# One block of attention, RWKV and feed-forward on one core: ascending queries, a fused output projection, weight sums made once

## The chip, the core and the metric

The kernel is one program on one core of a Trainium2 chip. The metric is the device time of one execution in microseconds (us); the change is timed against the kernel before on the same chip. The core's engines are PE (TensorE, matrix multiply), DVE (VectorE), ACT (ScalarE), POOL (GpSimd) and SP (SyncE, which only issues transfers here). Each takes its instructions in the order in which they stand in its queue; between engines there are semaphores. TensorE runs at one of two clocks, 2.4 or 1.2 GHz; the profile gives the granted clock of a stretch as a share of the full one.

## What is computed

2048 tokens of width 1024 pass through one block, all in float32:

```
u   = rmsnorm(x, attn_norm_pre)
p   = u @ w_in                            # queries, keys, values, gates; RWKV columns
o   = concat(forgetting_attention(p_fox), # 8 heads of 64, causal, log-gate bias
             rwkv7_time_mix(p_rwkv))      # 8 heads of 64, delta-rule state scan
h   = x + rmsnorm(o @ w_out, attn_norm_post)
z   = rmsnorm(h, ffn_norm_pre)
f   = (silu(z @ ffn_w_gate) * (z @ ffn_w_up)) @ ffn_w_down      # inner width 2816
out = h + rmsnorm(f, ffn_norm_post)
```

## The kernel before

Every float32 product is made of three matrix multiplications in a reduced format: an operand x is split into a high part (an ACT cast) and a low part (a DVE or POOL subtraction), and `mm3` adds high·high, high·low and low·high in PSUM (L78, L79 and L80). The big matrices are multiplied in blocks of two by two with seven products instead of eight, so that sums and differences of blocks have to be formed by DVE and POOL and split too. The Python code is written as generators that are woven together; a scheduler then orders the instructions of every engine, so that the order in an engine's queue is not that of the code.

The program runs in stages, told by the line of their TensorE work:

- Until about 805 us: input projection, its norms, and the operands of the RWKV scan.
- 805 to 1604 us (`phase_b`): the RWKV recurrence, woven with `attention`. Attention works head by head in units of 256 queries, J from 7 down to 0; unit J needs keys 0 to 256·(J+1). Keys (Ks), values (Vs) and gate sums (ng) come in four segments of 512 keys a head, the last segment first (L864 to L872). The heads' results go to a DRAM tensor, scr_mixT (L977 for attention, L780 for RWKV).
- 1604 to 1849 us (`Mix`): the output projection `passes` in four passes: columns 0 to 511 of the first 1024 tokens, columns 512 to 1023 of the same, then these two for the other tokens. Only one half of w_out is on chip, so that it is loaded and split three times (L1035 to L1046), and every tile of scr_mixT is loaded and split twice (`load`, L1049). A tile's result goes from PSUM through ACT (L1081) to a DRAM tensor, scr_mix. `norm` (L1087) reads a tile of 128 tokens back, makes both norms with an inverse square root by Newton steps on DVE (L61 to L63), adds x on POOL (L1111), writes h, and transposes z on TensorE (npt, L1121) into DRAM (scr_z). The first eight tiles are normed beside the projection, the last eight as side work of gate and up.
- 1849 to 2749 us (`Ffn.quad`): 44 quads of gate or up, each of 7 products of 12 multiplications (gp), 22 for each half of the tokens. `wprep` loads and splits the weights of the next quad (fraw, wh, wl); `zprep` builds the operands za, zb, zc of a half from scr_z, for the first half in `start` and `open`. The products of the quad go through four PSUM banks. The inner activations are written to a DRAM tensor, scr_hid (L1381).
- 2749 to 3299 us (`down`): for each half of the tokens, five chunks of two row pairs, and in a chunk 7 products × 4 tiles (dps) that are added up on DVE (L1574; those of the first chunk are copied by ACT, L1571), then a last pair (L1600) and the final norm. `down_prep` makes a chunk's operands: four loads of 1 MB each (L1436; two of scr_hid, two of w_down), sums s1 to s4 of the activations and t1 to t4 of the weights on DVE (L1482), then high parts (ACT, L1474) and low parts (POOL or DVE, L1476).

The sums t1 to t4 depend on the weights alone, and are formed for each half again:

```
            add(t1, b12, b11, ALU.subtract)     # L1498 and on: 2 adds a call
            ops(s1, t1)
            add(t3, b22, b12, ALU.subtract)
            ops(s3, t3)
```

Of the kernel before, what the change touches and what calls it, by code (L numbers as in the profile page):

```python
# [10 lines left out]
F32 = mybir.dt.float32  # L11
# [820 lines left out]
def attention(k, tc, ctx, scr):  # L832


# [23 lines left out]
    def load_head(h):  # L858
# [5 lines left out]
        def loads():  # L864
            for sgm in range(NS - 1, -1, -1):
# [144 lines left out]
class Mix:  # L1010


    def __init__(m, k, tc, ctx, ins, scr):
        m.k, m.nc, m.ins, m.scr = k, tc.nc, ins, scr
        m.pw = ctx.enter_context(tc.tile_pool(name="e_w", bufs=1, side="right"))
        m.pr = ctx.enter_context(tc.tile_pool(name="e_r", bufs=1, side="right"))
        m.w = [None] * NJ
        m.d = 0
        m.low = itertools.cycle([m.nc.gpsimd])
        m.rot = [(m.pr, f"r{i}") for i in range(3)]  # L1020

    def open(m, tc, ctx):

        m.pm = ctx.enter_context(tc.tile_pool(name="e_m", bufs=2, side="right"))
        m.pn = ctx.enter_context(tc.tile_pool(name="e_n", bufs=1, side="right"))
        m.low = itertools.cycle([m.nc.vector, m.nc.gpsimd])
        m.rot += [(m.pm, f"r{i}") for i in range(3, 8)]
# [6 lines left out]

    def weights(m):  # L1035

        nc = m.nc
        c = slice(m.d * 512, (m.d + 1) * 512)
        for j in range(NJ):
            h = m.pw.tile([128, 512], F32R, tag=f"wh{j}", name="ewh")  # L1040
            l = m.pw.tile([128, 512], F32R, tag=f"wl{j}", name="ewl")
            t = m.r([128, 512])
            nc.sync.dma_start(out=t, in_=m.ins["w_out"][0][j * 128:(j + 1) * 128, c])
            nc.scalar.copy(h, t)
            next(m.low).tensor_tensor(l, t, h, op=ALU.subtract)
            m.w[j] = h, l  # L1046
            yield

    def load(m, tt):  # L1049
        nc = m.nc  # L1050
        t = slice(tt * 128, (tt + 1) * 128)
        mh = m.pm.tile([128, NJ, 128], F32R, tag="mh", name="emh")
        ml = m.pm.tile([128, NJ, 128], F32R, tag="ml", name="eml")
        for i in range(2):
            c = slice(i * 4, (i + 1) * 4)
            r = m.r([128, 4, 128])
            nc.sync.dma_start(out=r, in_=m.scr["mixT"][i * 512:(i + 1) * 512, t].rearrange("(j p) t -> p j t", p=128))
            nc.scalar.copy(mh[:, c], r)
            next(m.low).tensor_tensor(ml[:, c], r, mh[:, c], op=ALU.subtract)
        return mh, ml  # L1060

    def passes(m, psum, done):

        nc = m.nc
        n = m.k.T // 256
        for i, half in enumerate((0, 0, 1, 1)):
            if i % 2 == 1:
                m.d = 1 - m.d
                for _ in m.weights():
                    pass  # L1070
            c = slice(m.d * 512, (m.d + 1) * 512)
            nxt = m.load(half * n)
            for tt in range(half * n, (half + 1) * n):
                mh, ml = nxt
                if tt + 1 < (half + 1) * n:
                    nxt = m.load(tt + 1)
                ps = psum.tile([128, 512], F32, tag="e", name="eps")
                for j, (wh, wl) in enumerate(m.w):
                    mm3(nc, ps, mh[:, j, :], ml[:, j, :], wh, wl, j == 0, j == NJ - 1)
                o = m.r([128, 512])  # L1080
                nc.scalar.copy(o, ps)  # L1081
                nc.scalar.dma_start(out=m.scr["mix"][tt * 128:(tt + 1) * 128, c], in_=o)
                if i % 2 == 1:
                    done[0] = tt + 1
                yield

    def norm(m, tt, pool, psum, bufs=1):  # L1087
# [3 lines left out]
        a = pool.tile([128, D], F32, tag="na", name="na", bufs=bufs)  # L1091
        nc.sync.dma_start(out=a, in_=scr["mix"][t, :])
        ss = pool.tile([128, 1], F32, tag="nss", name="nss", bufs=bufs)
        rs = pool.tile([128, 1], F32, tag="nrs", name="nrs", bufs=bufs)

        def factor():
            junk = pool.tile([128, D], BF16, tag="nr", name="njunk", bufs=2 * bufs)
            nc.scalar.activation(junk, a, AF.Square, accum_out=ss)
            nc.vector.tensor_scalar(ss, ss, 1.0 / D, NORM_EPS, op0=ALU.mult, op1=ALU.add)
            rsqrt(nc, pool, rs, ss, "nq")  # L1100

        factor()
        yield
        for d in range(2):
            c = slice(d * 512, (d + 1) * 512)
            g = pool.tile([128, 512], F32, tag="nr", name="ng", bufs=2 * bufs)
            nc.sync.dma_start(out=g, in_=m.ins["attn_norm_post"][0][c].partition_broadcast(128))
            nc.vector.scalar_tensor_tensor(a[:, c], a[:, c], rs, g, op0=ALU.mult, op1=ALU.mult)
            x = pool.tile([128, 512], F32, tag="nr", name="nx", bufs=2 * bufs)
            nc.sync.dma_start(out=x, in_=m.ins["x"][0, t, c])  # L1110
            nc.gpsimd.tensor_tensor(a[:, c], a[:, c], x, op=ALU.add)  # L1111
            yield
        nc.gpsimd.dma_start(out=scr["h"][t, :], in_=a)
        factor()
# [556 lines left out]
```

## Time and profile before

| | us |
|---|---|
| median of 3 runs | 3307.99 (3302.31 to 3308.15) |
| the profiled execution | 3300.75 |
| its span, first to last instruction | 3299.0 |
| TensorE busy in the span | 3032.2 (92%) |
| VectorE busy | 2434.5 (74%) |
| ScalarE busy | 1584.9 (48%) |
| GpSimd busy | 1383.9 (42%) |

The mean granted clock of TensorE was 0.961. An engine's busy share is an average over stages with different limits. A view that cuts the span into windows shows for each stage how long each engine worked in it; where TensorE stands below its window, the rows of its timeline tell in brackets how long it had been idle before an instruction, and which engine or transfer ended that. A row of the windows holds start and end, length, busy time (and number of instructions) of PE, PEld (TensorE's weight loads), DVE, ACT and POOL, then the granted clock, the busy share of the sixteen transfer engines and the GB/s that they moved. A group of instructions gives its count, its busy time with the mean of one in ns, and the idle time before its instructions with what ended it.

### The profile page before, as it was taken

How to read it: one execution, taken by the hardware profiler on the slowest of the kernel's cores; microseconds unless marked ns; L12 is line 12 of the kernel's file. 1: busy time of each engine (PE TensorE's matmuls, PEld its weight loads, DVE VectorE, ACT ScalarE, POOL GpSimd, SP SyncE). 2: the span in 40 equal slices, each digit the busy share in tenths (PEclk: the TensorE clock that was granted, in tenths of full speed). 3: DMA queues.
4: the chain of work that ended last, by engine and by line, in shares of the span. 5: the costliest groups of instructions: out<-in, count | busy, mean ns of one | idle time of the engine just before them, and what ended most of it. 6: DMA issues, size and time to landing. Idle time of an engine off the chain costs nothing. (4 is left out here: it accounts for less than half of the span.)

```text
span 3299.0 us, 48970 instructions
## 1 busy us (share of the span) xinstructions
PE 3032.2 (92%) x16913; PEld 2511.0 (76%) x16913; DVE 2434.5 (74%) x5129; ACT 1584.9 (48%) x3256; POOL 1383.9 (42%) x1031
## 2 busy tenths in 40 slices
PE   7999999998999999999797699999899999996895
PEld 5777777777888889988676578888788887774674
DVE  6876777675677777777545867877865657999898
ACT  5444534433677777777444434333333335333432
POOL 3444444443111111111334434444533336887786
PEclk9999999999999999999898899999999999998998
DMA  4766656668433333332377634442322224231321
GB/s 131 193 148 183 178 159 167 154 174 229 119 110 120 105 113 108 107 106 62 97 224 241 218 106 138 139 136 89 128 77 83 84 90 160 102 128 48 131 103 77
DMA packets 463629, 434.09 MB, mean 132 GB/s; under 512 B 138148, under 2 KB 379862, under 8 KB 461334
## 3 DMA queue, kind: packets, MB, share of 16 engines
q1 hardware_dynamic: 432262, 390.52, 39.0%
q10 hardware_dynamic: 24208, 20.52, 2.1%
q0 software_dynamic: 6912, 19.93, 2.0%
q8 instruction: 134, 2.20, 0.3%
q14 instruction: 113, 0.93, 0.1%
HBM read 304.11 MB, written 126.75 MB: 131 GB/s over the span
## 5 line engine op out<-in xcount | busy, mean ns | idle before, releaser
L255 POOL TENSOR_TENSOR wl<-wraw,wh 128x1024 fp32r<-128x1024 f32 (+1 forms) x108 | 263.4, 2443 | 286.9 <-ACT wh L254 283.7
L1231 POOL TENSOR_TENSOR wl<-fraw,wh 128x512 fp32r<-128x512 f32 x132 | 184.9, 1402 | 462.1 <-ACT wh L1227 447.5
L1476 POOL TENSOR_TENSOR dop<-draw,dop 128x512 fp32r<-128x512 f32 x210 | 331.5, 1610 | 101.2 <-ACT dop L1474 57.3
L1227 ACT CAST wh<-fraw 128x512 fp32r<-128x512 f32 x308 | 187.2, 618 | 387.7 <-PE gp L79 206.0
L78 PE MATMUL mm<-uh,wh 128*128 128x512 f32 (+1 forms) x864 | 347.2, 403 | 0.0
L80 PE MATMUL mm<-uh,wl 128*128 128x512 f32 (+1 forms) x864 | 344.4, 399 | 0.0
L79 PE MATMUL mm<-ul,wh 128*128 128x512 f32 (+1 forms) x864 | 343.4, 397 | 0.0
L78 PE MATMUL dps<-dop 128*128 128x512 f32 x624 | 251.2, 410 | 62.9 <-ACT acc L1571 26.2
L1474 ACT CAST dop<-draw 128x512 fp32r<-128x512 f32 x280 | 155.5, 620 | 231.8 <-DVE draw L1482 160.2
L79 PE MATMUL dps<-dop 128*128 128x512 f32 x624 | 248.9, 400 | 1.4 <-POOL dop L1476 1.4
L80 PE MATMUL dps<-dop 128*128 128x512 f32 x624 | 246.0, 398 | 0.1
L78 PE MATMUL gp<-za,wh 128*128 128x512 f32 x528 | 210.4, 398 | 21.4 <-ACT za L1227 15.5
L976 POOL TENSOR_TENSOR ot<-ot,rb 64x256 f32<-64x256 f32 x64 | 46.4, 726 | 428.2 <-ACT rb L975 428.2
L1231 DVE TENSOR_TENSOR wl<-fraw,wh 128x512 fp32r<-128x512 f32 x176 | 153.7, 873 | 86.6 <-ACT wh L1227 73.7
L955 DVE TENSOR_TENSOR tl<-pt,th 128x512 fp32r<-128x512 f32 (+1 forms) x280 | 163.2, 591 | 73.2 <-ACT th L953 69.6
L79 PE MATMUL gp<-za,wh 128*128 128x512 f32 x528 | 208.4, 395 | 1.2 <-DVE za L1231 1.2
L80 PE MATMUL gp<-za,wl 128*128 128x512 f32 x528 | 208.6, 395 | 0.0
L78 PEld LDWEIGHTS dps<-dop 128*128 128x128 f32 x624 | 121.0, 194 | 107.8 <-DVE acc L1574 35.0
L1482 DVE TENSOR_TENSOR draw<-draw 128x512 f32<-128x512 f32 x160 | 198.0, 1254 | 6.5 <-POOL dop L1476 6.0
L909 DVE CUSTOM_DVE_ANT_0 P<-S,ng 128x512 f32<-128x512 f32 (+2 forms) x320 | 183.6, 605 | 24.8 <-PE pt L947 13.9
L78 PEld LDWEIGHTS mm<-uh,wh 128*128 128x128 f32 (+1 forms) x864 | 164.6, 191 | 41.3 <-issue 3.5
L920 ACT ACTIVATE P<-P,nmx 128x896 f32<-128x896 f32 (+7 forms) x248 | 187.5, 761 | 14.4 <-DVE nmx L914 14.1
(376 smaller groups left out, 8554.1 us busy)
## 6 DMA issues: line engine op xcount, KB each, us to landing
wraw<-in_w_in SPq DMA_DIRECT2D x104, 512.0 KB
fraw<-in_ffn_w_gate SPq DMA_DIRECT2D x22, 1024.0 KB
fraw<-in_ffn_w_up SPq DMA_DIRECT2D x22, 1024.0 KB
scr_hid<-s SPq DMA_DIRECT2D x22, 1024.0 KB
draw<-scr_hid SPq DMA_DIRECT2D x22, 1024.0 KB
draw<-in_ffn_w_down SPq DMA_DIRECT2D x22, 1024.0 KB
scr_a<-A SPq DMA_DIRECT2D x16, 1280.0 KB
A<-scr_a SPq DMA_DIRECT2D x64, 320.0 KB
```

Of the source, the lines that this page charges most:

```text
L78: nc.tensor.matmul(out, lhsT=wh, rhs=xh, start=first, stop=False)
L79: nc.tensor.matmul(out, lhsT=wh, rhs=xl, start=False, stop=False)
L80: nc.tensor.matmul(out, lhsT=wl, rhs=xh, start=False, stop=last)
L255: nc.gpsimd.tensor_tensor(wl[:, :, 0:m], raw[:, :, 0:m], wh[:, :, 0:m], op=ALU.subtract)
L909: nc.vector.tensor_tensor_reduce(out=P[:, c0:c0 + n], in0=S[:, 0:n], in1=ng[c0 // 512][:, 0:n], op0=ALU.add, op1=ALU.max, scale=1.0, scala ...
L920: nc.scalar.activation(P[:, x0:x1], P[:, x0:x1], AF.Exp, bias=nmx, accum_out=ls[:, qi, i:i + 1])
L955: nc.vector.tensor_tensor(tl[:, w[0], w[1]], pt[:, w[0], w[1]], th[:, w[0], w[1]], op=ALU.subtract)
L1227: f.nc.scalar.copy(h, x)
L1231: e.tensor_tensor(l[:, c], x[:, c], h[:, c], op=ALU.subtract)
L1474: f.nc.scalar.copy(r[0][p][i], x)
L1476: e.tensor_tensor(r[1][p][i], x, r[0][p][i], op=ALU.subtract)
L1482: V.tensor_tensor(o[p], x[p], y[p], op=op)
```

## The change

Four parts are changed; the counts are of instructions in the built programs.

1. `attention`: units go from J = 0 to 7, segments are loaded from the first on; of the first head two segments are requested ahead, the others at J = 2 and 3, those of the next head at J = 4 and 6.
2. `Mix`: both halves of w_out are held on chip, split once (`others` brings the second half in during the first tiles). `project` takes two tiles of tokens at a time through both halves; each tile of scr_mixT is loaded and split once. The result stays in SBUF (na); squares are summed by ACT from PSUM; scr_mix is gone. The inverse root is ACT's square root with one Newton step (`rsqrt2`). All 16 tiles are normed beside the projection. The projection has PSUM banks of its own, three for eps and one for npt.
3. `Ffn`: gate, up and down use eight PSUM banks in turn (`bank`). The weights of the first quad are prepared in `open`. A new generator, `column_sums`, forms t1 to t4 for the five chunks of w_down once, as side work of gate and up: 20 units, each of two loads of 256 KB, four POOL sums of 128x256 elements and one store of 512 KB, the transfers too issued by POOL.
4. `down_prep`: the DVE sums t1 to t4 are gone, 80 of 160 (L1482). `column_loads` reads the seven weight operands of a chunk, 512 KB each, from w_down or from the stored sums (scr_wt), up to six ahead.

```diff
-            for J in range(NJU - 1, -1, -1):
+            for J in range(NJU):
...
-        for _ in units[0].hd.loads:
-            pass
+        next(units[0].hd.loads)
+        next(units[0].hd.loads)
...
-            if u is not None and u.J * QB % 512 == 0 and i + NJU < len(units):
+            if u is not None and u.J in (2, 3):
+                next(u.hd.loads)
+            elif u is not None and u.J in (4, 6) and i + NJU < len(units):
                 next(units[i + NJU].hd.loads)
...
+    def project(m, ready):
+        n = m.k.T // 128
+        ops = {tt: m.load(tt) for tt in range(2)}
+        others = m.others()
+        for p in range(0, n, 2):
...
+            for d in range(2):
+                for tt in (p, p + 1):
...
+                    ps = m.ps.tile([128, 512], F32, tag="e", name="eps")
...
+                    for j, (wh, wl) in enumerate(m.w[d]):
+                        mm3(nc, ps, mh[:, j, :], ml[:, j, :], wh, wl, j == 0, j == NJ - 1)
...
+                    nc.scalar.activation(junk, ps, AF.Square, accum_out=a[tt][1][:, d:d + 1])
+                    nc.scalar.copy(a[tt][0][:, c], ps)
+                    if d == 1:
+                        ready.append((tt, *a[tt]))
...
+    def norm(m, tt, a, s2):
...
+            nc.vector.scalar_tensor_tensor(a[:, c], a[:, c], rs, m.g[:, c], op0=ALU.mult, op1=ALU.mult)
+            nc.gpsimd.tensor_tensor(x[:, c], a[:, c], x[:, c], op=ALU.add)
+            nc.scalar.activation(junk, x[:, c], AF.Square, accum_out=s2[:, d:d + 1])
...
+    def bank(f, new=True):
+        f.nps += 1
+        return f.ps[f.nps % 2 if new else 0].tile([128, 512], F32, tag="g", name="gp")
...
+    def column_sums(f):
+        for fp in range(f.NP - 1):
+            for q in range(2):
+                x = f.pc.tile([128, 2, 2, 256], F32, tag="cs", name="csum")
+                for j in range(2):
+                    nc.gpsimd.dma_start(out=x[:, j], in_=w[fp, :, j]...)
+                yield
+                G.tensor_tensor(b11, b12, b11, op=ALU.subtract)
+                G.tensor_tensor(b12, b22, b12, op=ALU.subtract)
+                G.tensor_tensor(b22, b22, b11, op=ALU.subtract)
+                G.tensor_tensor(b21, b21, b22, op=ALU.subtract)
+                nc.gpsimd.dma_start(out=f.scr["wt"][fp, :, :, q * 256:(q + 1) * 256], ...)
+                yield
...
+            if q > 0:
+                side.append(itertools.islice(sums, 1 + (q % 2)))
...
+    def column_loads(f, seq):
+            for b in ("b11", "b21", 0, 1, 3, "b22", 2):
...
+                f.nc.sync.dma_start(out=x, in_=src.rearrange("f p c -> p f c"))
...
-            add(t1, b12, b11, ALU.subtract)
-            ops(s1, t1)
+            ops(s1)
...
-                pool, tag = ((f.psd, "d"), (f.ps, "g"))[nps[0] % 2]
+                ps = f.bank()
```

Where attention ends and the output projection begins, TensorE's queue held this before (O is attention's result, gp here the RWKV output gate, eps the projection, emh the split tile of scr_mixT):

```order
L78 MATMUL gp<-xl_16171,g1h 128x512
L79 MATMUL gp<-xl_16173,g1h 128x512
L80 MATMUL gp<-xl_16171,g1l 128x512
L778 MATMUL gp<-xl_16175,g2s 128x512
L965 MATMUL O<-th,Vs 128x256
L965 MATMUL O<-th,Vs 128x128
L969 MATMUL O<-ident,rl 64x128 x2
L78 MATMUL eps<-ewh,emh 128x512
L79 MATMUL eps<-ewl,emh 128x512
```

Now it holds this there (yT is the transpose that ends the recurrence):

```order
L964 MATMUL O<-th,Vs 128x128
L964 MATMUL O<-tl,Vs 128x128
L968 MATMUL O<-ident,rl 64x128 x2
L769 MATMUL yT<-ident,yg 128x128 x8
L78 MATMUL eps<-ewh,emh 128x512
L79 MATMUL eps<-ewl,emh 128x512
L80 MATMUL eps<-ewh,eml 128x512
```

The projection's first rows now stand ahead of the gate's, which come among them; before, the gate's last rows stood ahead of attention's last result.

VectorE's queue in a middle chunk of the down product held this before (draw is the result of a sum, dop a low part, acc the adding up):

```order
L1574 TENSOR_TENSOR acc<-dps,acc 128x512 x4
L1476 TENSOR_TENSOR dop<-draw,dop 128x512
L1482 TENSOR_TENSOR draw<-draw 128x512 x2
L1574 TENSOR_TENSOR acc<-dps,acc 128x512 x2
L1482 TENSOR_TENSOR draw<-draw 128x512
L1574 TENSOR_TENSOR acc<-dps,acc 128x512 x2
L1476 TENSOR_TENSOR dop<-draw,dop 128x512
L1482 TENSOR_TENSOR draw<-draw 128x512 x3
L1574 TENSOR_TENSOR acc<-dps,acc 128x512 x5
L1476 TENSOR_TENSOR dop<-draw,dop 128x512
L1574 TENSOR_TENSOR acc<-dps,acc 128x512 x2
L1482 TENSOR_TENSOR draw<-draw 128x512
```

Now it holds this in such a chunk:

```order
L1570 TENSOR_TENSOR draw<-draw 128x512
L1652 TENSOR_TENSOR acc<-gp,acc 128x512
L1570 TENSOR_TENSOR draw<-draw 128x512
L1652 TENSOR_TENSOR acc<-gp,acc 128x512 x2
L1564 TENSOR_TENSOR dop<-draw,dop 128x512
L1652 TENSOR_TENSOR acc<-gp,acc 128x512
L1570 TENSOR_TENSOR draw<-draw 128x512
L1652 TENSOR_TENSOR acc<-gp,acc 128x512
L1570 TENSOR_TENSOR draw<-draw 128x512
L1652 TENSOR_TENSOR acc<-gp,acc 128x512 x2
L1564 TENSOR_TENSOR dop<-draw,dop 128x512
L1652 TENSOR_TENSOR acc<-gp,acc 128x512 x4
```

The sums between the additions to acc came in groups of one to three, and come singly now.

SP's queue at the start of the down product held this before (scr_hid<-s is the store of the last activations):

```order
L1381 DMA scr_hid<-s 128x2x1024
L1436 DMA draw<-in_ffn_w_down 128x2x1024
L1436 DMA draw<-scr_hid 128x2x1024
L1436 DMA draw<-in_ffn_w_down 128x2x1024
L1436 DMA draw<-scr_hid 128x2x1024
L1436 DMA draw<-in_ffn_w_down 128x2x1024
L1381 DMA scr_hid<-s 128x2x1024
L1436 DMA draw<-scr_hid 128x2x1024
L1436 DMA draw<-in_ffn_w_down 128x2x1024 x2
L1436 DMA draw<-scr_hid 128x2x1024 x2
```

Now it holds this (dcol is a weight operand, scr_wt the stored sums):

```order
L1517 DMA dcol<-in_ffn_w_down 128x2x512
L1517 DMA dcol<-scr_wt 128x2x512 x3
L1498 DMA draw<-scr_hid 128x2x1024 x2
L1517 DMA dcol<-scr_wt 128x2x512
L1517 DMA dcol<-in_ffn_w_down 128x2x512 x3
L1419 DMA scr_hid<-s 128x2x1024
L1517 DMA dcol<-scr_wt 128x2x512 x3
L1498 DMA draw<-scr_hid 128x2x1024 x2
```

The last store of activations has moved behind the loads of two activation blocks and of four weight operands that are issued just ahead of it.

## Rows read from the trace of the kernel before

**Rows 1.** Windows by stage: busy us (x instructions) of PE, PEld, DVE, ACT, POOL; clock; transfers.

```profile
1604.00:1619.00 15.00, 0.26 (x3) 0.00 (x0) 4.29 (x6) 3.51 (x9) 4.80 (x6) 0.60 0.74 219
1619.00:1735.00 116.00, 111.01 (x464) 88.92 (x465) 50.25 (x106) 46.46 (x84) 42.21 (x32) 0.95 0.65 205
1735.00:1849.00 114.00, 92.75 (x383) 72.58 (x382) 72.60 (x193) 50.52 (x81) 55.52 (x41) 0.91 0.79 253
1849.00:1900.00 51.00, 26.08 (x88) 19.43 (x89) 42.77 (x46) 17.82 (x19) 25.26 (x10) 0.70 0.52 166
1900.00:2320.00 420.00, 414.75 (x1838) 339.29 (x1836) 313.18 (x491) 159.92 (x265) 177.43 (x128) 1.00 0.37 121
2320.00:2340.00 20.00, 12.59 (x36) 9.45 (x37) 20.00 (x14) 6.44 (x7) 13.44 (x5) 0.66 0.61 203
2340.00:2749.00 409.00, 408.77 (x1788) 335.24 (x1787) 259.56 (x326) 143.89 (x243) 154.56 (x113) 1.00 0.24 83
2749.00:2973.00 224.00, 209.61 (x882) 165.20 (x881) 208.65 (x238) 93.45 (x168) 183.55 (x113) 0.98 0.37 139
2973.00:3237.00 264.00, 219.40 (x885) 173.85 (x884) 242.25 (x306) 104.62 (x205) 200.21 (x129) 0.92 0.26 96
3237.00:3299.00 62.00, 27.11 (x113) 20.22 (x111) 57.90 (x109) 12.41 (x40) 31.89 (x21) 0.79 0.17 68
```

**Rows 2.** Timeline of TensorE at attention's start: start, length, instruction [idle before <-what ended it].

```profile
826.33 0.80 PE L904 MATMUL S<-Ks,Q 128*128 128x512 f32 x1 [5.95 <-DMA Ks<-scr_kS]
```

**Rows 3.** Timeline of SP's queue at the same place (two of its five Ks loads).

```profile
814.11 0.33 SPq L868 DMA_DIRECT2D Ks<-scr_kS  x1
...
820.01 0.89 SPq L868 DMA_DIRECT2D Ks<-scr_kS  x1
```

**Rows 4.** Timeline of all engines from attention's end to the projection.

```profile
1606.88 0.59 POOL L977 DMA_DIRECT2D scr_mixT<-ot  x1 [0.29 <-POOL ot L976]
...
1613.57 1.14 ACT L1227 CAST wh<-fraw 128x512 fp32r<-128x512 f32 x2 [7.90 <-DMA fraw<-in_ffn_w_gate]
...
1619.10 0.80 PE L78 MATMUL eps<-ewh,emh 128*128 128x512 f32 x1 [14.85 <-ACT emh L1058]
```

**Rows 5.** Timeline of TensorE: eight transposes of 128x128 in a row.

```profile
1598.07 1.12 PE L769 MATMUL yT<-ident,yg 128*128 128x128 f32 x8
```

**Rows 6.** Groups by line, 1604 to 1900 us: count | busy, mean ns | idle before.

```profile
L78 PE MATMUL eps<-ewh,emh 128*128 128x512 f32 x256 | 104.1, 408 | 21.1 <-ACT emh L1058 17.6 <-ACT er L1081 3.0 <-ACT ewh L1044 0.4
...
L1111 POOL TENSOR_TENSOR na<-na,nx 128x512 f32<-128x512 f32 x20 | 29.7, 1488 | 25.9 <-DVE na L1108 8.7 <-DVE nrs L63 5.7 <-issue 4.8
```

**Rows 7.** Groups by line over the whole span, ACT's table loads (one of six such rows).

```profile
L368 ACT ACT_TABLE_LOAD x4 | 5.1, 1283 | 0.1
```

**Rows 8.** Timeline of TensorE: waits at the start of gate and up, and between its halves.

```profile
1864.98 0.80 PE L78 MATMUL gp<-za,wh 128*128 128x512 f32 x1 [11.75 <-ACT za L1227]
...
2323.65 0.77 PE L78 MATMUL gp<-za,wh 128*128 128x512 f32 x1 [5.87 <-DVE tx L1372]
```

**Rows 9.** Groups by line, 1900 to 2749 us: POOL's low parts, and DVE waiting for POOL.

```profile
L1231 POOL TENSOR_TENSOR wl<-fraw,wh 128x512 fp32r<-128x512 f32 x126 | 176.1, 1399 | 444.9 <-ACT wh L1227 430.4 <-PE gp L79 6.1 <-DVE wl L1231 4.7
...
L1372 DVE TENSOR_TENSOR tx<-gp,tx 128x512 f32<-128x512 f32 x43 | 29.6, 689 | 73.1 <-POOL tx L1368 73.1
```

**Rows 10.** The page's transfers issued by POOL: count, KB each, median us to landing.

```profile
scr_h<-na POOLq DMA_DIRECT2D x16, 512.0 KB, 3.2
bv<-scr_bv POOLq DMA_DIRECT2D x16, 256.0 KB, 3.0
```

**Rows 11.** Groups by line in the down product, 2750 to 3299 us.

```profile
L1476 POOL TENSOR_TENSOR dop<-draw,dop 128x512 fp32r<-128x512 f32 x202 | 318.4, 1608 | 94.4 <-ACT dop L1474 50.5 <-PE dps L80 25.2 <-DVE fss L1540 16.3
L78 PE MATMUL dps<-dop 128*128 128x512 f32 x624 | 251.2, 410 | 62.9 <-ACT acc L1571 26.2 <-DVE acc L1574 25.7 <-DVE acc L1600 5.5
...
L1482 DVE TENSOR_TENSOR draw<-draw 128x512 f32<-128x512 f32 x152 | 186.4, 1242 | 6.4 <-POOL dop L1476 6.0
L1474 ACT CAST dop<-draw 128x512 fp32r<-128x512 f32 x268 | 148.7, 620 | 222.8 <-DVE draw L1482 152.9 <-PE dps L80 51.4 <-issue 10.7
```

More of the change, by code (lines that the diff above doesn't have):

```diff
@@ L864, in loads @@
         def loads():
-            for sgm in range(NS - 1, -1, -1):
+            for sgm in range(NS):
                 c = slice(sgm * 512, (sgm + 1) * 512)
@@ L1055, in load @@
             c = slice(i * 4, (i + 1) * 4)
[L1056 to L1057 removed]
+            r = m.raws.pop((tt, i))
             nc.scalar.copy(mh[:, c], r)
[L1059 removed]
+            (nc.vector, nc.gpsimd)[i].tensor_tensor(ml[:, c], r, mh[:, c], op=ALU.subtract)
         return mh, ml
[L1062 removed]
+    def project(m, ready):
@@ L1064, in passes @@
         nc = m.nc
[L1065 to L1085, printed above, removed]
@@ L1092, in norm @@
[L1092 to L1100, printed above, removed]
@@ L1112, in norm @@
             yield
-        nc.gpsimd.dma_start(out=scr["h"][t, :], in_=a)
-        factor()
+        nc.gpsimd.dma_start(out=scr["h"][t, :], in_=x)
+        rs = m.factor(s2)
         yield
-        nc.scalar.activation(a, a, AF.Identity, scale=rs)
+        nc.scalar.activation(a, x, AF.Identity, scale=rs)
+        yield
         for jj in range(2):
-            pt = psum.tile([128, 4, 128], F32, tag="e", name="npt")
+            pt = m.pt.tile([128, 4, 128], F32, tag="t", name="npt")
             for q in range(4):
@@ L1125, in norm, with norms @@
             yield
-    def norms(m, tiles, pool, psum, bufs=1):
-        tiles = list(tiles)
-        for i in range(0, len(tiles), bufs):
-            yield from woven_steps(*(m.norm(tt, pool, psum, bufs) for tt in tiles[i:i + bufs]))
+    def norms(m, ready, done):
+        for tt in range(m.k.T // 128):
+            while not ready:
+                yield
+            yield from m.norm(*ready.pop(0))
+            done[0] = tt + 1
 def behind(tc, gen):
@@ L1402, in gate_up @@
             elif last:
-                for _ in late:
+                for _ in chain(late, sums):
                     pass
@@ L1444, in down_prep, with column @@
         f.dops = []
+        cols, ahead = f.column_loads(seq), []
+        def column():
+            ahead.extend(itertools.islice(cols, len(f.bslots) - len(ahead)))
+            return ahead.pop(0)
         nxt = f.down_load(*seq[0])
+        ahead.extend(itertools.islice(cols, len(f.bslots)))
         yield
@@ L1622, in fox_rwkv7_block, with start @@
         mix.open(tc, ce)
-        done = [0]
-        n = T // 256
-        def first():
-            while done[0] < 2:
+        ready, done = [], [0]
+        n = T // 128
+        def start():
+            while done[0] < n // 2:
                 yield
-            for i in range(0, n, 2):
-                while done[0] < i + 2:
-                    yield
-                yield from mix.norms(range(i, i + 2), mix.pn, ffn.psn, 2)
             yield from ffn.start()
-        weave((mix.passes(ce.enter_context(tc.tile_pool(name="e_q", bufs=2, space=PSUM)), done), 4 * n), (first(), 11 + n // 2 * 6 + 14, 0.95))
+        weave((mix.project(ready), 8 * n), (mix.norms(ready, done), 8 * n), (start(), 8 * n))
         ce.close()
-        ffn.open()
-        ffn.gate_up(mix.norms(range(n, 2 * n), ffn.pn, ffn.psn))
+        ffn.open(c2)
+        ffn.gate_up(iter(()))
         ffn.down()
```

192 lines of the change are left out of this document (122 added, 70 removed).

## The prediction

> **What bounds the kernel now.** I read first the windows by stage, then TensorE's timeline where a window shows it idle, then the groups by line for what it waits for, last the transfers. In the windows [rows 1] TensorE is busy for all of gate and up: 408.77 of 409 us from 2340, and 1788 instructions there give 408.77 / 1788 = 0.2287 us for one matrix multiplication at the full clock. Nothing on another engine can gain there. The time that TensorE doesn't use lies in four places: 15 us of nothing between attention and projection, the projection and the start of gate and up (1619 to 1900), 20 us between the halves of gate and up, and the down product, where DVE is busy 208.65 of 224 and 242.25 of 264 us. The change touches all four and adds work to gate and up. So it is priced as TensorE's loss, the length of a stretch less its multiplications at 0.2287 us, stage by stage. All sums are made against the profiled execution: 3300.75 us, a span of 3299.0 and 1.75 around it; the median of the runs shown is 3307.99, 7 us more.
>
> **Attention.** At its start TensorE waits 5.95 us for a key segment [rows 2]. That segment is the fourth that SP requests, at 820.01; the first is requested at 814.11 [rows 3]. Ascending, the first unit needs the first segment, 5.9 us earlier. That gains 0 to 6 us; I take 3, since the scan beside it had TensorE waiting for other things too. At the other end TensorE idles 14.85 us [rows 4]: the last result is stored at 1606.88, is then read back behind a megabyte of gate weights (its cast starts at 1613.57), and the first eps runs at 1619.10. Now tile 0 is read back ahead, and its cast waits only for the last store: 0.6 us of issue, the 2.2 to 3.2 us that such stores take to land, 0.6 for a cast, and eps can start about 1611, 8 earlier. But the transposes yT, which in the queue of before had come before the last results, now stand behind them, ahead of eps; the norm that they wait for may be late. I take 4 of the 8, with a loss of 2 at worst and a gain of 11 at best. Together −7 us (+2 to −17).
>
> **Projection to the end of gate and up.** From 1619.10 to the last gp at 2749.4 there are 1130.3 us. The code has 16 tiles × 2 halves × 8 blocks × 3 = 768 eps and 44 quads × 84 = 3696 gp, in all 4464 × 0.2287 = 1020.9, and 128 transposes at 1.12 / 8 = 0.14 us [rows 5], 17.9: 1038.9 us. So 91.4 us are lost. By the windows [rows 1], idle time is 26.2 in 1619 to 1849, 24.9 in 1849 to 1900, 5.3 in 1900 to 2320, 7.4 in 2320 to 2340 and 0.2 after, 64.0 us; the other 27.4 are multiplications that ran slower, in the windows with granted clocks of 0.91, 0.70 and 0.66.
>
> What goes: the waits for emh, 17.6 us [rows 6], 14.85 of them the one counted above, and others of that kind; the second and third loading and splitting of w_out; half of the tile loads (16 instead of 32, with their casts and subtractions); and the round trip of scr_mix, in the stretch where transfers stood at 0.79 [rows 1]. What comes: eight more tiles of norms beside the projection. They are no new work, since they ran in gate and up before. Per tile they cost POOL 2 × 1.49 us [rows 6] and ACT two squares more. At 768 × 0.2287 / 16 = 11 us of TensorE a tile, ACT and POOL have room: they are busy 46 and 42 of 116 us in the first window. Square root and silu switch ACT's tables, five loads more at 1.28 us [rows 7], hidden in the same room.
>
> At the start of gate and up TensorE idled 11.75 us for za's cast [rows 8] and more for zb and zc. In the new queue part of quad 0 stands between the last eps, so that some of that is filled; but the operands zc wait until all norms have ended, and the norms of tiles 14 and 15 have no projection left to hide them. I put the loss there at 20 us (10 to 40). The rest of after: 5 for a start at low clock, 12 in the course of the projection and of gate and up, 8 between the halves, where the wait for tx is 5.87 [rows 8] and eight banks instead of four let TensorE run ahead. That is 45 against 91.4: −46 us (−15 to −70).
>
> **Column sums.** Twenty units, 80 POOL sums. A 128x512 subtraction takes POOL 1399 ns in this stretch [rows 9]; half the elements about 0.7 us. A unit is 4 × 0.7 and three issues of 0.59 [rows 4], 4.6 us. A quad lasts 84 × 0.2287 = 19.2 us and takes three quarters of a unit on average (1 + q mod 2 steps of two), 3.4 us; POOL is busy 177.43 of 420, so 8.1 of 19.2. With 11.5 of 19.2 it has room, and DVE, which waits 73.1 us for POOL's tx [rows 9], is off TensorE's path there. The sums wait for their loads, though, at the head of POOL's queue, and the low parts wl of the next quad and tx of this one stand behind. POOL's transfers of 256 KB land after 3.0 us, of 512 KB after 3.2 [rows 10]. With about 6 us of such waits a unit, 4.5 a quad, POOL is at 16 of 19.2. I take 0, from 0 to +20.
>
> The Trainium skill ("SBUF — State Buffer", section "SBUF: two separate sides") speaks against this part: transfers issued from GpSimd need descriptors that GpSimd cannot write while VectorE holds their shared port in a two-port mode, and an operation with two SBUF inputs on VectorE locks out GpSimd for its whole length. The landings here don't show that, with DVE busy 313 of 420 us and medians of 3.0 and 3.2. By the rule the waits would be longer, and the slower case below is how that would decide.
>
> **The down product.** The loss by windows [rows 1]: 224 − 882 × 0.2287 = 22.3; 264 − 885 × 0.2287 = 61.6; 62 − 113 × 0.2287 = 36.2. In the groups TensorE's waits are for additions to acc by ACT and DVE, and ACT waits 152.9 us for DVE's draw sums [rows 11]. Eighty of 160 sums go, at 1.242 us [rows 11], 99 us of DVE, half in each half of the tokens. In the second stretch DVE falls from 242 to 242 − 40 × 1.242 = 193 of 264, below TensorE's 202. POOL with 200.21 then stands nearest to TensorE. Its 1608 ns [rows 11] against 1399 in gate and up [rows 9] is what the same subtraction costs beside a busier DVE, so it should fall by some of the 0.2. I leave a loss of 25 there: −37. The tail is a chain of sums that stay: 0. In the first stretch the steady loss falls to a few us, but a wait is new. The first copy to acc on ACT uses space that the last activations held, and waits for their store, which SP has now behind loads of 2 MB of activations and 2 MB of weights. At the 253 GB/s of the busiest window [rows 1], 4 MB take 17 us, 28 with the 3 MB of residuals and norm weights. Behind the copy on ACT stand the casts of the next operands. TensorE has eight banks × 6 × 0.2287 = 11 us before it stops for it. So 0 to 19, I take 10: the loss is 14 instead of 22.3, −8. The weight loads grow from 2 to 3.5 MB a chunk, in a stage where transfers stood at 0.37 and 0.26 [rows 1]; up to six are ahead, so I count nothing for them. Together −45 us (−15 to −84).
>
> On that store the Trainium skill ("DMA: Bandwidth & Descriptors", section "Queues, rings and completion order") says that each transfer engine consumes one issuer's descriptors in ring order. By it the store would pay all that SP requested before it, the 17 us and not less; the trace of before has no store behind such a row of loads. Where the requests are spread thinner it would cost nothing, 10 us less than the sum.
>
> **Sum.** −7 − 46 + 0 − 45 = −98: 3300.75 − 98 = 3203 us, and with part of the 7 us to the median I say 3205. The bounds of the parts don't fall together; the likeliest case has 3185 to 3228.
>
> **The rivals.** POOL takes DVE's place in the down product: for it speak its 200.21 busy and 1608 ns; against it, that ACT waits for DVE's sums and not for POOL. Then TensorE keeps some 50 of its 61.6 us loss, the down product gives −8 − 12 = −20, and the time is 3228. Chance 0.18.
>
> The norms don't fit beside the projection: each is a chain through four engines, POOL's na waited 25.9 us [rows 6], and TensorE's transposes stand in its queue among eps. If they hold it, the second term gives −10 instead of −46: 3239. Against it speak the low busy shares there. Chance 0.14.
>
> All of it comes off: no wait at the down product's start, 20 us less loss in DVE's stretch: −98 − 10 − 20 = −128, 3173. Chance 0.10.
>
> Slower: POOL's queue stops at each column sum for its transfers. From gate and up on POOL, 8.1 + 3.4 of 19.2 us are work, and 7.7 a quad or 10.3 a unit are free. To lose the 98 us on 20 units each must wait 10.3 + 4.9 = 15.2 us, two landings of 7.6 where 3.0 and 3.2 are seen [rows 10]; from 9 us on it is slower, 20 × (18 − 10.3) = +154 against −98: 3357. Chance 0.08.
>
> **Chances.** Likeliest case 0.50, and the four 0.18, 0.14, 0.10 and 0.08. The measurement tells 0.2%, some 7 us, from no change. Faster: the first four cases hold 0.92; 0.05 of that goes to a milder form of the last one, which eats up the gain: 0.87 faster, 0.04 within, 0.09 slower. The range holds the likeliest case, the first two rivals and most of the high one: 3160 to 3270.
>
> **What would show it.** Right: DVE in the second half of the down product under 0.8 busy and TensorE over 0.88; under 25 us idle from the last eps to the third quad; TensorE at 0.98 or more through gate and up with POOL at 0.6. Wrong: TensorE idle for tx or wl in gate and up (POOL's queue), for npt or emh in the projection, or POOL over 0.9 in the down product. A first copy of acc later than some 11 us after the first dps confirms the new wait. If gate and up grow by more than 20 us, the whole forecast is wrong.

## The result, and the profile after

The changed kernel takes 3326.26 us (median of 6 runs) against 3307.99: a ratio of 1.0054, 95% interval 1.004 to 1.0069. It is half a per cent slower; 98 us less had been forecast. The profiled execution has a span of 3324.7 us, 25.7 more than before; between the medians it is 18, since the profiled execution of before lies 7 us under its median. Cut at the same places of the work, this is where they lie (positions of first and last instructions from the two traces):

| stretch | before | after | difference | forecast |
|---|---|---|---|---|
| start to the first eps | 1619.1 | 1638.0 | +18.9 | −7 |
| first eps to the first product of down | 1130.5 | 1169.7 | +39.2 | −46 (sums of columns 0 in it) |
| down, first product to the end | 549.4 | 516.9 | −32.5 | −45 |

So one of three terms came, smaller than said, and two have the wrong sign. These are the windows of the changed kernel, with the columns of [rows 1], cut at its own stages:

```profile
1627.00:1638.00 11.00, 2.82 (x15) 2.01 (x15) 8.16 (x34) 3.12 (x8) 5.45 (x6) 0.67 0.66 244
1638.00:1754.00 116.00, 101.68 (x424) 81.87 (x423) 50.94 (x111) 51.14 (x112) 47.97 (x34) 0.91 0.50 161
1754.00:1868.00 114.00, 85.49 (x343) 66.97 (x342) 43.66 (x109) 40.52 (x94) 32.24 (x25) 0.85 0.38 123
1868.00:1905.00 37.00, 33.30 (x151) 26.62 (x150) 17.14 (x38) 12.62 (x31) 11.75 (x9) 1.00 0.32 106
1905.00:1960.00 55.00, 25.31 (x74) 17.99 (x73) 34.20 (x56) 28.46 (x44) 23.95 (x17) 0.63 0.31 105
1960.00:2380.00 420.00, 415.82 (x1804) 337.42 (x1803) 296.10 (x318) 137.69 (x235) 263.37 (x247) 1.00 0.39 132
2400.00:2807.00 407.00, 405.33 (x1764) 330.16 (x1763) 258.47 (x326) 145.53 (x247) 154.89 (x114) 1.00 0.24 83
3031.00:3260.00 229.00, 201.93 (x848) 162.82 (x849) 202.42 (x262) 101.55 (x204) 188.27 (x124) 0.94 0.40 138
```

The projection, 1638 to 1905, is where the most is lost. TensorE is busy 85.49 of 114 us in its second window, while ACT is busy 40.52, DVE 43.66 and POOL 32.24, and transfers stand at 0.38 where [rows 1] had 0.79. No engine is full, and TensorE waits: that is a chain of waits, not a lack of room. The granted clock falls to 0.91 and 0.85 over those gaps, so the multiplications between them are slower as well.

What TensorE waited for, from attention's end to the end of gate and up (waiting instruction <- releaser: us in all, times, longest):

```profile
PE eps L78 <- ACT na L1118: 34.3, 15, 4.6
PE npt L1156 <- ACT na L1150: 27.0, 4, 13.1
PE npt L1156 <- DVE nz L1158: 10.3, 8, 4.6
PE yT L769 <- POOL yg L764: 8.2, 2, 7.9
```

L1118 is the copy of a result out of PSUM, which frees its bank for the next eps. What ACT waited for in the projection:

```profile
ACT njunk L1117 <- DMA scr_z<-nz: 63.8, 15, 9.3
ACT emh L1084 <- PE eps L79: 29.5, 12, 5.3
ACT njunk L1145 <- POOL nx L1143: 19.5, 11, 3.3
```

The first row is the key. L1117 squares a result out of PSUM; it writes its squares into a scratch tile, njunk, that nobody reads. That tile has the tag "nz" (a tag names the buffers that tiles take in turn), and so shares two buffers with nz, the normed tile that is stored to scr_z. The square waits until a store of nz has landed, and the copy stands behind the square in ACT's queue. ACT's timeline shows one such case, TensorE's the next:

```profile
1677.92 0.60 ACT L1117 ACTIVATE njunk<-eps 128x512 bf16<-128x512 f32 x1 [7.79 <-DMA scr_z<-nz]
1678.41 0.20 ACT L1117 ACTIVATION_READ_ACCUMULATOR njunk<-eps 128x1 f32 x1
1678.51 0.58 ACT L1118 COPY na<-eps 128x512 f32<-128x512 f32 x1
```

```profile
1691.88 0.60 PE L1156 MATMUL npt<-ident,na 128*128 128x128 f32 x4
1695.24 0.51 PE L78 MATMUL eps<-ewh,emh 128*128 128x512 f32 x1 [2.76 <-ACT na L1118]
```

ACT stands still for 7.79 us ahead of a 0.60 us square. In TensorE's queue the transposes npt, from which nz is made, stand among the eps that wait for ACT, so that a late square delays the next nz and its store as well.

In gate and up TensorE is at 415.82 of 420 and 405.33 of 407 us. POOL rose from 177.43 [rows 1] to 263.37 us, and its waits for the column sums' transfers, in 1960 to 2380, are these:

```profile
POOL csum L1433 <- DMA scr_wt<-csum: 23.7, 15, 2.9
POOL csum L1436 <- DMA csum<-in_ffn_w_down: 20.1, 18, 2.3
POOL csum L1437 <- DMA csum<-in_ffn_w_down: 11.3, 13, 2.8
```

The twenty units of sums, whose subtractions all fall in this stretch, cost POOL 55 us of waits; TensorE's waits for DVE's results of the quads come to 2.5 us from 1960 to 2807. At the start of the down product the new wait is there, on TensorE and ACT, with ACT's and SP's issues ahead of it (three timelines; fht is the residual, loaded for the final norm):

```profile
2832.89 0.80 PE L78 MATMUL gp<-dop 128*128 128x512 f32 x1 [14.07 <-ACT acc L1649]
```

```profile
2808.36 11.31 ACTq L1612 DMA_DIRECT2D fht<-scr_h  x4
2819.79 0.62 ACT L1562 CAST dop<-draw 128x512 fp32r<-128x512 f32 x1 [12.80 <-DMA draw<-scr_hid]
...
2832.26 4.50 ACT L1649 COPY acc<-gp 128x512 f32<-128x512 f32 x9 [4.11 <-DMA scr_hid<-s]
```

```profile
2808.52 0.87 SPq L1498 DMA_DIRECT2D draw<-scr_hid  x2
2809.45 0.64 SPq L1517 DMA_DIRECT2D dcol<-scr_wt  x1
2814.16 9.22 SPq L1517 DMA_DIRECT2D dcol<-in_ffn_w_down  x3
2823.47 0.42 SPq L1419 DMA_DIRECT2D scr_hid<-s  x1
```

Down starts at 2807.8; the last store of activations is issued only at 2823.47, and the first copy runs at 2832.26. Nine copies run in one row then; TensorE had stopped at 2818.8, the 11 us after its first product that eight banks had been counted for. ACT's row of loads of fht spans 11.31 us, and its last one waits, by the trace, for the same landing of draw as the cast behind it.

### The profile page after: what moved, and what is told of

Same layout as the page of the kernel before. It is cut to its first block, busy times and chain, and to the rows that moved or that the text cites. A ratio compares the mean times of both kernels' runs of the same rounds, so it can differ in the third digit from the quotient of the medians.

```text
span 3324.7 us, 48795 instructions
## 1 busy us (share of the span) xinstructions
PE 3032.5 (91%) x16913; PEld 2516.5 (76%) x16913; DVE 2315.3 (70%) x4837; ACT 1576.3 (47%) x3317; POOL 1439.5 (43%) x1151
## 5 line engine op out<-in xcount | busy, mean ns | idle before, releaser
L78 PE MATMUL gp<-dop 128*128 128x512 f32 x624 | 247.7, 400 | 47.4 <-ACT acc L1649 28.6
L79 PE MATMUL gp<-dop 128*128 128x512 f32 x624 | 246.8, 396 | 0.0
L80 PE MATMUL gp<-dop 128*128 128x512 f32 x624 | 243.4, 394 | 0.0
L1564 POOL TENSOR_TENSOR dop<-dcol,dop 128x512 fp32r<-128x512 f32 x140 | 207.4, 1486 | 73.7 <-ACT dop L1562 44.3
L1271 DVE TENSOR_TENSOR wl<-fraw,wh 128x512 fp32r<-128x512 f32 x176 | 161.3, 916 | 99.9 <-ACT wh L1267 94.8
L919 ACT ACTIVATE P<-P,nmx 128x128 f32<-128x128 f32 (+7 forms) x248 | 187.7, 761 | 14.8 <-DVE nmx L913 14.6
L80 PEld LDWEIGHTS mm<-uh,wl 128*128 128x128 f32 (+1 forms) x864 | 165.1, 191 | 37.2 <-issue 0.2
L79 PEld LDWEIGHTS mm<-ul,wh 128*128 128x128 f32 (+1 forms) x864 | 164.4, 190 | 36.9 <-issue 1.5
L964 PE MATMUL O<-th,Vs 128*128 128x256 f32 (+1 forms) x672 | 181.7, 326 | 9.1 <-ACT rb L974 7.8
```

Source lines behind the costliest of these rows:

```text
L78: nc.tensor.matmul(out, lhsT=wh, rhs=xh, start=first, stop=False)
L79: nc.tensor.matmul(out, lhsT=wh, rhs=xl, start=False, stop=False)
L80: nc.tensor.matmul(out, lhsT=wl, rhs=xh, start=False, stop=last)
L919: nc.scalar.activation(P[:, x0:x1], P[:, x0:x1], AF.Exp, bias=nmx, accum_out=ls[:, qi, i:i + 1])
L964: nc.tensor.matmul(O[:, q0 * 128:QB], lhsT=vv, rhs=p[:, e, q0:NQ, :], start=kb == 0 and i == 0, stop=kb == nkb - 1 and i == len(parts) - 1)
L1271: e.tensor_tensor(l[:, c], x[:, c], h[:, c], op=ALU.subtract)
```

## The experiments

**njunk in space of its own.** The two scratch tiles get a tag that no stored tile has:

```diff
-                    junk = m.pn.tile([128, 512], BF16, tag="nz", name="njunk")
+                    junk = m.pn.tile([128, 512], BF16, tag="nj", name="njunk")
```

> The changed kernel (3326 us) with the squares' scratch tile njunk in space of its own instead of the space of nz. Theory 1: in the projection ACT's square waits for the store of nz to DRAM (63.8 us in its trace), the copy na behind it frees the PSUM bank, and TensorE waits for that copy 34.3 us; then these waits go, the stretch from first eps to the first down product falls from 1169 to about 1130 us, total about 3287. Rival: the norm chain through ACT, DVE and POOL is as long as the projection anyway; then the wait moves to npt or to the emh casts and the total stays within 10 us of 3326.

Measured: 3255.41 us, ratio to before 0.9846 (0.983 to 0.9861), 71 us less than the changed kernel and more than the waits of 34.3 that went. From the first eps to the first product of down it is 1097.7 us instead of 1169.7. TensorE's waits from 1638 to 1832, all of them:

```profile
PE yT L769 <- POOL yg L764: 8.3, 2, 7.8
PE npt L1156 <- DVE nz L1158: 0.5, 1, 0.5
PE npt L1156 <- ACT na L1150: 0.3, 1, 0.3
```

The windows of the projection and of the change to gate and up:

```profile
1640.00:1756.00 116.00, 115.14 (x527) 94.25 (x526) 63.16 (x148) 64.36 (x145) 56.66 (x41) 0.99 0.62 193
1756.00:1831.00 75.00, 75.00 (x355) 61.92 (x354) 48.25 (x116) 40.23 (x97) 37.82 (x26) 1.00 0.56 181
1831.00:1887.00 56.00, 32.48 (x132) 24.98 (x131) 46.57 (x50) 27.51 (x39) 33.73 (x22) 0.76 0.42 135
```

TensorE is busy 190.1 of 191 us at 0.99 and 1.00, with 104 of the 128 transposes npt before the last eps: 13 of the 16 tiles are normed beside the projection. The last three follow in the window from 1831, where TensorE waits 21.6 us for npt. So the rival falls: the chain of a norm fits beside the projection, and what held it was two buffers. The stretch gains 72 us where the waits for the copy were 34.3: TensorE's idle time in it falls from 88.9 to 42.4 us, since the waits for npt fell too, and the other 25.5 us are multiplications that ran faster, the clock of the projection having risen from 0.91 and 0.85.

**Attention in descending order, in the changed kernel, and ascending in the kernel before.** Two kernels; the first undoes part 1 of the change, the second makes it alone. The key loads go with the order in both; of the first this is the line of the order:

```diff
-            for J in range(NJU):
+            for J in range(NJU - 1, -1, -1):
```

> The changed kernel (3326 us) with attention back in descending order of queries, loads with it. Theory 1: the ascending order itself costs the 19 us by which the projection now starts later (1638.0 against 1619.1); then it starts near 1616 and the total is about 3305. Rival: the later start comes from other parts (operands fetched ahead, space, the transposes yT behind the last results); then the first eps stays near 1635 and the total near 3326.

> The kernel before (3308 us) with only the attention in ascending order. Theory 1: last O moves from 1603.8 to about 1625 and the total to about 3328. Rival: the ascending order costs only beside the new output projection; then the total is 3308 less up to 6 us for the key segment at attention's start.

Measured: 3317.92 us, ratio 1.0039 (1.0027 to 1.0052), and 3325.26 us, ratio 1.0061 (1.0048 to 1.0073). In the kernel before, the ascending order with its loads costs 22 us (3303.23 was the median of the kernel before in the same session), more than the whole change lost. The last O ends at 1623.3 there instead of 1604.3; from the first O on that is 779.2 us against 755.7 before. In the changed kernel the descending order brings the last O from 1628.0 to 1608.1, but the first eps only from 1638.0 to 1624.0, since tile 0 is then what the last units produce:

```profile
PE eps L78 <- ACT emh L1082: 15.9, 1, 15.9
```

In the descending order the changed kernel's first unit waits 5.0 us for its keys; in the ascending one TensorE is idle 7.6 us before its first S, with no releaser in the profile. The 5.95 us [rows 2] that were to be had there didn't come. The new order of loads isn't what costs the 22 us: behind that first S, TensorE waits for no transfer in the attention of either ascending kernel.

**The last store of activations from POOL's queue**, past SP's row of loads:

```diff
-            nc.sync.dma_start(out=f.scr["hid"][...], in_=...)
+            (nc.gpsimd if q == f.NQUAD - 1 else nc.sync).dma_start(out=f.scr["hid"][...], in_=...)
```

> The changed kernel (3326 us) with the last store of activations issued by POOL instead of SP. Theory 1: the first copy of acc waits for that store, which SP issues only at 2823.5 behind loads; then TensorE's wait of 14.07 us there goes and the total falls by 10 to 14 us, to about 3314. Rival: the store is late because the transfer engines are full of what was requested before, whoever issues it; then the wait stays at 10 us or more and the total within 5 us of 3326.

Measured: 3326.85 us, ratio 1.0063 (1.0047 to 1.008): nothing. ACT's timeline there:

```profile
2819.84 0.62 ACT L1562 CAST dop<-draw 128x512 fp32r<-128x512 f32 x1 [12.67 <-DMA draw<-scr_hid]
...
2829.39 1.14 ACT L1562 CAST dop<-dcol 128x512 fp32r<-128x512 f32 x2 [2.97 <-DMA dcol<-in_ffn_w_down]
2830.43 4.48 ACT L1649 COPY acc<-gp 128x512 f32<-128x512 f32 x9
```

The store is issued at 2817.79, 5.7 us earlier, and the copy waits for it no longer. It now stands behind the casts ahead of it in ACT's queue, whose operands land as late; TensorE waits 12.18 us. Theory 1 had the right wait and not the one behind it.

**The tile s on the other side of SBUF**, so that acc doesn't lie on its space; on top of the first experiment:

```diff
-        f.pt = f.cw.enter_context(tc.tile_pool(name="f_t", bufs=1, side="right"))
+        f.pt = f.cw.enter_context(tc.tile_pool(name="f_t", bufs=1))
```

> The changed kernel with njunk in space of its own (3255 us), and the pool of the activations' tile s on the other side of SBUF, so that acc doesn't lie on its space. Theory 1: the first copy of acc then need not wait for the last store nor stand behind the casts that the scheduler put ahead of it; TensorE's wait of 14.2 us at the down product's start falls under 3 and the total to about 3243. Rival: the operands of products 5 to 7 wait for their loads there anyway; then TensorE waits for a cast in its place, and the total stays within 4 us of 3255.

Measured: 3225.91 us, ratio 0.9757 (0.9743 to 0.9772), 29 us less than without. The scheduler now puts the first copies between the casts; ACT at the start of down, which is at 2726.6:

```profile
2729.33 0.57 ACT L1649 COPY acc<-gp 128x512 f32<-128x512 f32 x1
2729.58 0.33 ACTq L1612 DMA_DIRECT2D fht<-scr_h  x1
2729.80 0.58 ACT L1649 COPY acc<-gp 128x512 f32<-128x512 f32 x1
```

The first half of down falls from 238.5 to 222.5 us, which is 16 of the 29. Another 7 lie between the first eps and down. The first eps is 4 us earlier too, which I take for scatter: it lies between 1633.6 and 1640.0 in the five traces that have the ascending order and the same code up to there. In the first half of down the edit freed more than the copy. The loads of fht in ACT's queue, the last of which had waited until 2819.3 in the changed kernel, wait for nothing here and are all issued by 2729.9. So the 16 us belong to the copy, to its place before the casts and to these loads together; no run tells them apart.

**Eighty VectorE operations put back in the place of the sums**, on top of the first experiment. Each is the maximum of a stored sum with itself, so that the data stays the same (code shortened):

```diff
+                if col:
+                    for p in range(NPR):
+                        V.tensor_tensor(b[:, p], b[:, p], b[:, p], op=ALU.max)
```

> The changed kernel with njunk in space of its own (3255 us), with 80 VectorE operations put back in the down product: a maximum of each of the four stored sums with itself, 128x512 in place, ahead of its cast. The data stays the same. Theory 1: VectorE's sums were what the down product lost by; its length from the first product, 516 us, goes back towards the 550 of before, total about 3280. Rival: the gain came from the eight banks and from loading operands singly; then it stays under 522 us and the total under 3262.

Measured: 3283.86 us, ratio 0.9943 (0.993 to 0.9957), 28 us more, though the first eps is 6 us earlier in this trace, within the scatter just named. Down goes from 516.3 to 553.2 us, even above the 549.4 of before. The groups of the down product, TensorE's wait first, then the 80 operations (78 in the window) and the sums that had stayed:

```profile
L78 PE MATMUL gp<-dop 128*128 128x512 f32 x624 | 252.6, 408 | 70.6 <-ACT acc L1652 29.4 <-DVE acc L1655 24.5 <-ACT dop L1565 9.1
...
L1560 DVE TENSOR_TENSOR dcol<-dcol 128x512 f32<-128x512 f32 x78 | 105.6, 1392 | 10.3 <-DMA dcol<-scr_wt 8.0 <-POOL dop L1567 2.2
L1573 DVE TENSOR_TENSOR draw<-draw 128x512 f32<-128x512 f32 x76 | 82.3, 1093 | 0.3
```

DVE's acc is back as a releaser with 24.5 us, as in [rows 11]. So VectorE's load is enough to explain the gain of the down product: eighty operations take all of it back. Whether the banks and the loads gain anything beside it, no run shows.

**Attention descending, and descending with the last head ascending**, both on top of the first experiment. The second, its loads in the same order:

```diff
-            for J in range(NJU):
+            for J in range(NJU) if h == NH - 1 else range(NJU - 1, -1, -1):
```

> The changed kernel with njunk in space of its own (3255 us) and attention in descending order. Theory 1: the descending order gives back 3.6 us a head, about 20 us at the last result O, and takes 8 us at the boundary, where tile 0 then waits for the last unit; so about 3243. Rival: the 11 us that the descending order gave beside the shared space are lost now to another wait; then 3255.

> The changed kernel with njunk in space of its own (3255 us), heads 0 to 6 in descending order and only the last head ascending. Theory 1: both orders' gains together: last O near 1612, no wait for emh of 16 us at the boundary; about 3237. Rival: the boundary waits for the end of the recurrence (yg) whatever the order; then the time is that of all heads descending, within 4 us.

Measured: 3233.97 us, ratio 0.9787 (0.9774 to 0.9799), and 3223.96 us, ratio 0.9759 (0.9747 to 0.9772). The mixed order has the short way of the descending one (756.3 us from first to last O) and a wait of 3.8 us at the boundary instead of the descending one's 16.3. Its first eps is at 1618.5, against 1640.0 ascending and 1626.7 descending.

**What in the ascending order costs.** Two more, on top of the first experiment. One takes the units of a head in the order 0, 2, 4, 6, 7, 5, 3, 1, with the keys loaded ahead; the other changes one weight with which the recurrence is woven in:

```diff
-        weave((recurrence([0]), NB * (8 * 10 + 13), 0.85), ...
+        weave((recurrence([0]), NB * (8 * 10 + 13), 0.7), ...
```

> The changed kernel with njunk in space of its own (3255 us, last O at 1629.5) and each head's units in the order 0, 2, 4, 6, 7, 5, 3, 1, keys loaded ahead. Theory 1: the ascending order loses at the change of heads, where the large values of J = 7 stand beside the small scores of J = 0 and TensorE waits for their chain; a small unit beside a small one removes that: last O near 1610, total about 3235. Rival: it loses at every step in which the next unit's scores are larger than the values beside them; half of the steps here are such, and last O lies near 1620, the total near 3246.

> The changed kernel with njunk in space of its own (3255 us), and the recurrence woven in earlier beside the ascending attention (its weight 0.7 instead of 0.85). Theory 1: in ascending order the recurrence is drawn out to the very end of attention, its last Y at 1628 beside the last O at 1629, and TensorE's 99.5 us a head come from that mixture; with the recurrence ahead, last O comes before 1620 and the total falls by 12 us or more. Rival: the loss a head lies in attention's own chain (the low parts of the large units on VectorE); then the heads still take 98 us or more on average, and only the wait of 7.8 us for yg at the end goes: about 3247.

Measured: 3269.76 us, ratio 0.989 (0.9874 to 0.9905), and 3244.56 us, ratio 0.9823 (0.9799 to 0.9846). The first fell out beyond both theories: its last O ends at 1650.6, later than the ascending 1629.8. So it isn't the change of heads alone. TensorE's largest wait in it, and the same in the second kernel:

```profile
PE pt L946 <- DVE tl L954: 22.9, 19, 2.4
```

```profile
PE pt L946 <- DVE tl L954: 12.3, 18, 1.6
```

In the changed kernel that wait is 13.6 us, in the kernel before 3.9. It is for the low part of a unit's probabilities on DVE (tl), which only the units from J = 3 on have. With the recurrence ahead, a head takes 97.9 us on average instead of some 98.1, and the last O comes at 1619.4 because the recurrence's part of the last head has gone; that is between the two theories. The 11 us between this kernel and the first experiment are at the edge of the noise, since the intervals of the two ratios meet. Over the second to the seventh head the orders took 95 us a head descending, 98 ascending and 102 in the third; TensorE's idle time in these heads is 1.8, 4.6 and 6.8 us a head. Eight heads at 2.8 us more would be 22 us, an estimate from these figures. Which neighbours in the queues make that difference stays open.

**The three edits together**: njunk apart, mixed order, s on the other side.

> The changed kernel with the three edits together: njunk in space of its own, heads 0 to 6 descending and the last ascending, the activations' tile s on the other side of SBUF. Theory 1: they act in different stages and add up: 3326 - 70 - 31 - 29 gives about 3196. Rival: an earlier end of one stage meets a later one's transfers (weights of the down product, column sums); then it stays above 3210.

Measured: 3207.02 us, ratio 0.9704 (0.9688 to 0.972), 3% faster than before. Its projection and its first half of down:

```profile
1616.00:1806.00 190.00, 189.40 (x871) 155.73 (x872) 110.60 (x260) 105.28 (x241) 95.63 (x67) 0.98 0.59 188
...
2704.00:2927.00 223.00, 215.75 (x938) 176.77 (x937) 193.60 (x232) 100.97 (x191) 181.57 (x119) 0.98 0.51 175
```

It is 11 us above theory 1's sum, and under the rival's 3210. Theory 1 counted something twice: between first eps and down, mixed order and side of SBUF each gain some 10 and 7 us over the first experiment, and together 9.7. What that gain is stays open. The stretch is 1087 to 1091 us in all six traces that change attention's order, the weaving or the side, and 1098 to 1099 in the two others with njunk apart.

## Why the prediction was wrong

- **What bounds the kernel**: the reading by windows held. Gate and up are TensorE's in both kernels, and the time was to be had where it was sought: the three edits bring the 3205 that had been forecast, to 2 us, from the same three stretches (−2.6, −42.5 and −48.7 against −7, −46 and −45). That it comes within 2 us is luck: in that kernel seven of eight heads descend, where the forecast had all ascend, and that order costs 22 us in the kernel before.
- **Projection to the end of gate and up, −46: the step that failed** is "ACT and POOL have room: they are busy 46 and 42 of 116 us". They had room, and the first experiment shows that the norms fit. But the step asked how long the engines work, not for what the new instructions wait and which buffers they write to. The square that the change puts between a result and its copy shares its space with a tile on its way to DRAM: 63.8 us of waits on ACT, 34.3 on TensorE, +39.2 in place of −46. Without the sharing the stretch is −32.8: the term was right in kind and 13 us too large. Those 13 are spread. By the prediction's own count, length less multiplications, the first experiment loses some 28 us in the window from 1831, which has 23.5 us idle (20 had been put for it, and 5 for a low clock), 10 between the halves (8), and 19 in the course of the projection and of gate and up (12). (408.77 / 1788 is 0.2286, not 0.2287, which is under half a microsecond in the stretch.)
- **The rival with the norms** named "a chain through four engines" and was priced at 36 us less. Of the four it came nearest to what happened in this stretch, and was wrong in its cause: beside the projection it was not the chain's length but one buffer of it. In time the fourth, 3357, lay nearer to 3326, but what it named, POOL's queue stopping TensorE in gate and up, did not happen.
- **Attention, −7**: the sign was wrong. The sum looked at both ends, 5.95 and 14.85 us, and took the units between them to take the same time in either order. They don't: +22 us in the kernel before with only the order and its loads changed. The boundary itself, from the last O's end to the first eps, fell from 14.8 us to 10.0, about as taken. The order of the units was taken as a reordering of the same instructions at no cost; here, where units and a scan share the queues, it has one, and its cause stays open. This is the second step that failed.
- **Column sums, 0**: right for the changed kernel. POOL waited 55 us for transfers in 1960 to 2380, and TensorE stayed at 415.82 of 420; the medians to landing were 3.4 us for loads and 3.3 for stores. They may cost something all the same: DVE's waits for POOL's tx in 420 us rose from 28.8 to 50.1 us, and in the first experiment TensorE waits 8.0 us for DVE's ty from 1887 to 2307. No run takes the sums alone away. The Trainium skill's warning of starved descriptors ("SBUF — State Buffer", section "SBUF: two separate sides") is for VectorE's two-port modes; these medians show no starving, with DVE busy 296.10 of 420 us, but no run shows whether an operation here was in such a mode. The lock by two SBUF inputs, which the prediction put beside it, that section limits to GpSimd operations that read SBUF.
- **Down, −45**: −32.5, in the range. The wait at its start was taken at 10 and is 14.07 us; its first cause (the store) was told apart by one experiment from what stands behind it (casts and loads ahead on ACT), and a second freed both. The order that the Trainium skill gives for one ring ("DMA: Bandwidth & Descriptors", section "Queues, rings and completion order") is not shown by itself: with the store on POOL's queue something else was late. The second half gained 25.7 instead of 37: TensorE still loses in its first chunk, where it waits for ACT's copies (11.84 us at 3084.2), and DVE is at 202 us of 229, not at 193 of 264. The sums that stay became longer, 1368 ns in the first experiment's trace against 1242 [rows 11].
- **The forecast signs**: a first copy later than 11 us after the first product (24.5) confirmed the wait; TensorE idle for npt in the projection was named as a sign of the forecast being wrong, and it was. TensorE at 0.99 through gate and up with POOL at 0.63 came as said; DVE under 0.8 in the second half of down did not (0.88).

## What to carry to other kernels

Before pricing an edit by busy shares, list for every new instruction the buffer it writes and who last held that buffer, scratch that nobody reads too: here a write into space that a DMA still read waited like a true dependence, and all that stood behind it on its engine waited with it. When a stage shows no full engine and TensorE waits, follow the releasers back one engine at a time; here it took two views. A reordering of loop iterations is a change of its own: time it alone.

## What the runs showed that I had not expected

- One shared tag was worth 71 us of 3326, more than twice the 34.3 us that TensorE's trace puts down to the copy.
- Taking away one cause at the start of down moved the time by nothing, since the next wait stood 2 us behind; only the edit that freed the whole row ahead of the copy gave 16 us there.
- A VectorE sum of two SBUF operands, 128x512, took 1242 ns in the kernel before, 1368 with half of the sums gone, and 1093 with 80 other operations put back. Its mean moves with what runs beside it, from which cause no run shows, so here a count times a mean was good only to some 10%.
